# A decoder layer's gate and up projections as Strassen block products: one Trainium2 core

## The chip, the core and the metric

One core of a Trainium2 chip. The metric is device microseconds (us) of one execution. The kernel is written with a tile framework: the program gives instructions in an order of priority, and a scheduler that knows each tile's readers and writers fixes, before the run, the order of instructions on every engine and DMA queue and puts in the semaphores.

## The reference

One layer of a hybrid decoder (two attention kinds, cross-attention into memory tokens, a feed-forward block) on 1024 prompt tokens and 8 sample tokens. What the change touches is the end of it, with D_MODEL = 1024 and D_FF = 2816:

```python
x = x + mem_attend(rmsnorm(x, xattn_norm_g), mem_k, mem_v, w_mq, mq_norm_g, w_mo)
hf = rmsnorm(x, ffn_norm_g)
x = x + (jax.nn.silu(hf @ w_gate) * (hf @ w_up)) @ w_down
```

## The kernel before

Activations lie transposed in SBUF: `xT` is [128 features, 8 blocks, 1032 tokens] in f32. Precision is kept by splitting every operand into a high and a low part (fp32r), and each product of 128 x 128 weights with a group of tokens is three matmuls into one PSUM bank (`proj`, L128): high by high, high by low, low by high. Tokens come in groups of 512, 256 and 264 (`GROUPS2`). A weight tile goes by `load_w` (L112): a DMA on SP's queue into `raw`, a copy on ACT (`wh`, L124) and a subtraction on GpSimd (`wl`, L125), with two buffers of each. `split` (L141) makes the halves of an activation with a copy on ACT and a subtraction on VectorE.

After the attention part, `stage_mem` (L1706) runs four kinds of generators that take turns (`run`): `mem_q`, `mem_attend` (as `both`), `mem_out`, and `mem_sample` for the sample tokens. `mem_out` (L1634) multiplies by `w_mo`, adds to `xT` (`residual`, L1484, with a running sum of squares `sqacc` on GpSimd, L1490), and for each group calls `scaled` (L1492): AH and AL become the halves of `xT` times the gain (L1498 on ACT, L1499 on VectorE), and a matmul of the squares, an Ln and an Exp give `rs`, the row of 1/rms. The norm is applied late: `gate_up` (L1734) multiplies each PSUM result by `rs` (L1745, L1753). So matmuls can start before `rs` is there.

D_FF is 22 tiles f of 128 columns. `gate_up(f)` makes 3 x 8 matmuls for each token group, first with `w_gate`, then with `w_up`; then SiLU (ACT), a product, and `split` into a tile for the down projection. The first 512 tokens of f = 0 to 3 are done beside `both(2, 3)` and `mem_sample`, their other groups after `mem_out(1, 2)`. `stage_ffn` (L1788) then alternates: `down` (L1758) of up to four finished tiles f (for each of 8 output blocks o a weight tile, three groups, one addition each into `xT`, L1767), and `gate_up` of the next four. The last chunk has two tiles f; in it `store_y` (L1771) transposes each finished block o back and stores it.

Of the kernel before, what the change touches and what calls it, by code (L numbers as in the profile page):

```python
# [6 lines left out]
F32 = mybir.dt.float32  # L7
FR = mybir.dt.float32r
# [5 lines left out]
OP = mybir.AluOpType  # L14
AX = mybir.AxisListType
PSUM = bass.MemoryType.PSUM
# [3 lines left out]
T = 1024  # L20
NS = 8
NT = T + NS
KD = D // 128
GROUPS = ((0, 384), (384, 384), (768, 264))
GROUPS2 = ((0, 512), (512, 256), (768, 264))
UW = 1040
EPS = 1e-6
BIG = 1e30
# [6 lines left out]
def f32(ap):  # L35
    return ap.bitcast(F32)


class Kernel:
    def __init__(self, tc, ins, outs):  # L40
        self.tc, self.nc, self.i, self.o = tc, tc.nc, ins, outs
        self.side, self.G = [], GROUPS
        self.set, self.set_users = None, []


    def mm(self, out, lhsT, rhs, start, stop):
# [5 lines left out]
    def unit(self, name, shape=None, dt=F32):  # L52
        return self.u.tile(shape or [128, UW], dt, name=name, tag="u")

# [1 line left out]
        return self.fp.tile(shape or [128, 388], dt, name=name, tag="f")  # L56

    def bt(self, name, shape=None):
        return self.hp.tile(shape or [128, 512], F32, name=name, tag="b", bufs=self.nB)

    def ht(self, name, shape=None, dt=F32):
        return self.hp.tile(shape or [128, 512], dt, name=name, tag="h")
# [1429 lines left out]
    def scaled(self, g, gain, rs):  # L1492

        nc = self.nc
        g0, n = self.G[g]
        s = slice(g0, g0 + n)
        for k in range(KD):
            nc.scalar.activation(self.AH[:, k, s], self.xT[:, k, s], AF.Copy, scale=gain[:, k:k + 1])  # L1498
            nc.vector.scalar_tensor_tensor(self.AL[:, k, s], self.xT[:, k, s], gain[:, k:k + 1], f32(self.AH[:, k, s]),  # L1499
                                           op0=OP.mult, op1=OP.subtract)  # L1500
        p = self.bank("sc", "pnt")
# [204 lines left out]
    def stage_mem(self):  # L1706


        self.omh, self.oml, self.mq = [self.AH[:, t] for t in range(2)], [self.AL[:, t] for t in range(2)], {}
        self.run([self.stage_out(0), 1.0, 0], [self.stage_mem_kv(), 1.2, 0])  # L1710
        self.run([self.stage_out(1, 2), 1.0, 0], [chain(self.mem_q(0), self.both(0, 1)), 0.4, 0])
        self.run([self.mem_q(1, 2), 1.0, 0], [self.mem_out(0), 1.5, 0])
        self.acts = [{} for _ in range(4)]
        gate_up = lambda *g: chain(*(self.gate_up(f, a, *g) for f, a in enumerate(self.acts)))

        def room(a, *groups):
            u, c = self.unit("a2", [128, 2, 520], FR), 0
            for g in groups:
                n = self.G[g][1]
                a[g] = u[:, 0, c:c + n], u[:, 1, c:c + n]  # L1720
                c += n

        for a in self.acts:
            room(a, 0)
# [3 lines left out]
        self.ub, self.u = self.u, self.tc.alloc_tile_pool(name="uC", bufs=10)  # L1728
        for a in self.acts:
            room(a, 1, 2)  # L1730
        self.run([gate_up(1, 2), 1.0, 0])


    def gate_up(self, f, act, *groups):  # L1734
        nc, V = self.nc, self.nc.vector
        cs = slice(128 * f, 128 * f + 128)
        gw = self.load_w(self.i["w_gate"][0][:, cs], KD, 128)
        uw = self.load_w(self.i["w_up"][0][:, cs], KD, 128)
        sgs = {}
        for g in groups:  # L1740
            g0, n = self.G[g]
            p = self.bank("mm", "pg")
            self.proj(*gw, 0, 128, g, p)
            sgs[g] = sg = self.bt("sg")
            V.tensor_mul(sg[:, :n], p[:, :n], self.rs[:, g0:g0 + n])  # L1745
            self.silu(sg[:, :n], sg[:, :n])
            yield
        for g in groups:
            g0, n = self.G[g]
            p = self.bank("mm", "pu")  # L1750
            self.proj(*uw, 0, 128, g, p)
            a = self.bt("a")
            V.tensor_mul(a[:, :n], p[:, :n], self.rs[:, g0:g0 + n])  # L1753
            V.tensor_mul(a[:, :n], a[:, :n], sgs[g][:, :n])
            self.split(a[:, :n], *act[g])
            yield

    def down(self, f0, acts, last):  # L1758
        nc, V = self.nc, self.nc.vector
        kt = len(acts)  # L1760
        for o in range(KD):
            wh, wl = self.load_w(self.i["w_down"][0][128 * f0:128 * (f0 + kt), 128 * o:128 * o + 128], kt, 128)
            for g, (g0, n) in enumerate(self.G):
                p = self.bank(("sc", "sk")[g % 2], "pd")
                self.proj(wh, wl, 0, 128, g, p, kt=kt, act=lambda k: acts[k][g])
                x = self.xT[:, o, g0:g0 + n]
                V.tensor_add(x, x, p[:, :n])  # L1767
            if last:
                self.store_y(o)

    def store_y(self, o):  # L1771
        nc = self.nc
        cs = slice(128 * o, 128 * o + 128)
        for half in range(2):
            p = self.bank(("tp", "sk")[half], "py")
# [3 lines left out]
            y = self.ub.tile([128, 4, 128], F32, name="y", tag="u")  # L1779
            (nc.vector.tensor_copy if half else nc.scalar.copy)(y, p.rearrange("p (t c) -> p t c", c=128))  # L1780
            nc.sync.dma_start(self.o["y_prompt"][0, 512 * half:512 * half + 512, cs].rearrange("(t p) c -> p t c", p=128), y)
        p = self.bank("tp", "py")
        self.tr(p[:NS, :128], self.xT[:, o, T:NT], 128)
        y = self.bt("y", [NS, 128])
# [3 lines left out]
    def stage_ffn(self):  # L1788
        F, C = 22, 4

        def gate_up(f):
            h, l = self.unit("ah", None, FR), self.unit("al", None, FR)
            act = [(h[:, g0:g0 + n], l[:, g0:g0 + n]) for g0, n in self.G]
            for _ in self.gate_up(f, act, 0, 1, 2):
                pass
            return act

        acts, f0 = self.acts, 0
        while f0 < F:
            n = len(acts)  # L1800
            nxt = []
            if f0 + n < F:
                nxt.append(gate_up(f0 + n))
            self.down(f0, acts, f0 + n >= F)
            f0 += n
            while nxt and len(nxt) < C and f0 + len(nxt) < F:
                nxt.append(gate_up(f0 + len(nxt)))
            acts = nxt


    def build(self):
        tc, nc = self.tc, self.nc
        P = tc.alloc_tile_pool
# [58 lines left out]
        self.nb = {"mm": 3, "tp": 1, "sc": 2, "sk": 2}  # L1872
        self.ps = P(name="psB", bufs=1, space=PSUM)
        self.wp = P(name="wB", bufs=1, side="right")
        self.keep = P(name="keepB", bufs=1)
# [4 lines left out]
        self.nB, self.G = 6, GROUPS2  # L1880
        self.u = P(name="uB", bufs=5)
# [5 lines left out]
        self.stage_ffn()  # L1887
        for p in (self.wp, self.u, self.ub, self.hp, self.sm, self.keep, self.act, self.c, self.dr, self.ps):
            p.release()

    def sample_gen(self):
# [33 lines left out]
```

## Time and profile before

| what | value |
|---|---|
| median of 3 runs | 1818.66 us (1818.63 to 1819.53) |
| the profiled execution | 1817.93 us, its span 1816.2 us |
| mean granted TensorE clock | 0.963 |
| busy: PE, PEld, DVE, ACT, POOL | 93%, 81%, 57%, 46%, 36% of the span |
| moved by DMA | 151.42 MB, 83 GB/s on average |

PE is TensorE's matmuls, PEld its weight loads (beside the matmuls), DVE is VectorE, POOL is GpSimd, SP issues most DMAs. A record of a matmul is longer than its share of the array, since matmuls are pipelined: what one costs is read from the distance between starts. The feed-forward block takes the last 800 us, and the engine that matters there is read from the view by stretches and the chain of waits.

### The profile page before, as it was taken

The numbers are of one execution on the slowest core, as the hardware profiler recorded it, in microseconds if no ns is written. First come the engines' busy times: TensorE is split into PE (matmuls) and PEld (weight loads), VectorE is DVE, ScalarE is ACT, GpSimd is POOL, SyncE is SP. The second block draws the span as 40 slices with busy tenths as digits, with TensorE's granted clock in tenths as the row PEclk, the third lists the DMA queues.
The fourth block names the chain that finished last, engine by engine and source line by source line (L and its number), as shares of the span: only waits on it lengthen the run. The fifth ranks groups of instructions, "written<-read, shape, count | busy, mean of one in ns | idle before, by whom it ended". The sixth has DMA issues, their size and how long they took to land.

```text
span 1816.2 us, 30619 instructions
## 1 busy us (share of the span) xinstructions
PE 1681.2 (93%) x11316; PEld 1471.5 (81%) x11316; DVE 1042.8 (57%) x2813; ACT 836.4 (46%) x2033; POOL 659.6 (36%) x641
## 2 busy tenths in 40 slices
PE   6998998767869999989998999999999999999998
PEld 5997887656747777767887779999999999999997
DVE  6799997999769877752366355323323323323324
ACT  5667879763446667645566563112112112112112
POOL 1376663445148133225454444222122122122121
PEclk9999998868989999989999999999999999999999
DMA  4133343323342334356222322121121121121013
GB/s 153 50 107 112 112 148 122 105 71 108 123 123 64 80 81 113 100 156 172 83 82 59 93 78 74 46 61 47 33 61 47 31 64 47 30 64 47 30 50 108
DMA packets 229855, 151.42 MB, mean 83 GB/s; under 512 B 29621, under 2 KB 216202, under 8 KB 229698
## 3 DMA queue, kind: packets, MB, share of 16 engines
q1 hardware_dynamic: 210906, 120.38, 22.9%
q0 software_dynamic: 4864, 14.69, 2.8%
q10 hardware_dynamic: 13936, 14.40, 2.3%
q8 instruction: 89, 1.46, 0.3%
q14 instruction: 60, 0.49, 0.1%
HBM read 118.77 MB, written 30.76 MB: 82 GB/s over the span
## 4 chain that ended last, share of the span: by engine, by line
PE 68%; DVE 11%; issue 3%; ACT 2%; DMA 1%; POOL 0%; SPq 0%; ACTq 0%; DVEq 0%; POOLq 0%
PE pu L47 14%; PE pd L47 14%; PE pg L47 14%; PE pm L47 8%; PE po L47 2%; PE pch L47 2%; PE plg L47 2%; PE pt L50 2%; DVE sk_junk L1266 2%; DVE AL L1499 1%; PE halves L47 1%; DVE tkj L349 1%; PE pmq L47 1%; PE pmo L47 1%; PE pmk L47 1%
## 5 line engine op out<-in xcount | busy, mean ns | idle before, releaser
L125 POOL TENSOR_TENSOR wl<-raw,wh 128x1024 fp32r<-128x1024 f32 (+3 forms) x153 | 311.9, 2039 | 745.8 <-ACT wh L124 741.0
L124 ACT CAST wh<-raw 128x1024 fp32r<-128x1024 f32 (+3 forms) x153 | 137.9, 901 | 311.9 <-PE pd L47 200.0
L47 PE MATMUL pm<-AH,wh 128*128 128x384 f32 (+7 forms) x792 | 270.1, 341 | 7.2 <-ACT wh L124 4.0
L47 PE MATMUL pm<-AL,wh 128*128 128x384 f32 (+7 forms) x792 | 263.4, 333 | 0.1
L47 PE MATMUL pm<-AH,wl 128*128 128x384 f32 (+7 forms) x792 | 262.3, 332 | 0.1
L47 PE MATMUL pg<-AL,wh 128*128 128x512 f32 (+2 forms) x528 | 169.7, 322 | 3.2 <-DVE AL L1499 3.1
L47 PE MATMUL pg<-AH,wh 128*128 128x512 f32 (+2 forms) x528 | 169.9, 322 | 1.1 <-DVE a L1753 1.1
L1767 DVE TENSOR_TENSOR xT<-xT,pd 128x512 f32<-128x512 f32 (+2 forms) x144 | 73.1, 512 | 169.5 <-PE pd L47 168.9
L47 PE MATMUL pu<-AL,wh 128*128 128x512 f32 (+2 forms) x528 | 169.5, 321 | 0.0
L47 PE MATMUL pu<-AH,wh 128*128 128x512 f32 (+2 forms) x528 | 169.4, 321 | 0.0
L47 PE MATMUL pu<-AH,wl 128*128 128x512 f32 (+2 forms) x528 | 168.8, 320 | 0.0
L47 PE MATMUL pg<-AH,wl 128*128 128x512 f32 (+2 forms) x528 | 168.8, 322 | 0.0
L47 PEld LDWEIGHTS pm<-AH,wh 128*128 128x128 f32 (+1 forms) x792 | 154.6, 195 | 15.3 <-ACT wh L124 5.4
L47 PEld LDWEIGHTS pm<-AL,wh 128*128 128x128 f32 (+1 forms) x792 | 154.4, 195 | 6.9 <-issue 1.3
L47 PEld LDWEIGHTS pm<-AH,wl 128*128 128x128 f32 (+1 forms) x792 | 153.6, 194 | 5.9 <-issue 1.1
L47 PE MATMUL pd<-ah,wh 128*128 128x512 f32 (+2 forms) x432 | 139.2, 323 | 0.0
L47 PE MATMUL pd<-al,wh 128*128 128x512 f32 (+2 forms) x432 | 138.3, 320 | 0.0
L47 PE MATMUL pd<-ah,wl 128*128 128x512 f32 (+2 forms) x432 | 137.7, 320 | 0.0
L1745 DVE TENSOR_TENSOR sg<-pg,rs 128x256 f32<-128x256 f32 (+2 forms) x66 | 34.0, 515 | 151.0 <-PE pg L47 142.3
L47 PEld LDWEIGHTS pg<-AL,wh 128*128 128x128 f32 x528 | 100.1, 190 | 11.8 <-DVE AL L1499 4.3
L47 PEld LDWEIGHTS pg<-AH,wh 128*128 128x128 f32 x528 | 100.0, 189 | 9.5 <-DVE a L1753 1.4
L1753 DVE TENSOR_TENSOR a<-pu,rs 128x256 f32<-128x256 f32 (+2 forms) x66 | 34.0, 516 | 128.2 <-PE pu L47 128.2
(647 smaller groups left out, 4196.8 us busy)
## 6 DMA issues: line engine op xcount, KB each, us to landing
raw<-in_w_gate SPq DMA_DIRECT2D x26, 512.0 KB
raw<-in_w_up SPq DMA_DIRECT2D x26, 512.0 KB
raw<-in_w_in SPq DMA_DIRECT2D x24, 512.0 KB
raw<-in_w_down SPq DMA_DIRECT2D x40, 256.0 KB
raw<-in_w_out SPq DMA_DIRECT2D x16, 512.0 KB
scrG<-y ACTq DMA_DIRECT2D x32, 192.0 KB
x<-in_x_prompt SPq DMA_DIRECT2D x8, 512.0 KB
xn<-in_x_prompt SPq DMA_DIRECT2D x8, 512.0 KB
```

What stands on the lines that cost most here:

```text
L47: return self.nc.tensor.matmul(out, lhsT, rhs, start=start, stop=stop)
L50: return self.nc.tensor.transpose(out, in_, self.ident[:p, :p])
L124: self.nc.scalar.copy(wh, raw)
L125: self.nc.gpsimd.tensor_sub(wl, raw, f32(wh))
L349: V.tensor_scalar(junk()[:, :(i + 1) * 128], data[i], t[:, j:j + 1], None, op0=op, op1=OP.add, accum_out=cnt[:, j:j + 1])
L1266: V.tensor_scalar(junk[:, j % 4, :N], data[:, :N], t, None, op0=op, op1=OP.add, accum_out=cnt[:, j:j + 1])
L1499: nc.vector.scalar_tensor_tensor(self.AL[:, k, s], self.xT[:, k, s], gain[:, k:k + 1], f32(self.AH[:, k, s]), op0=OP.mult, op1=OP.subtract)
L1745: V.tensor_mul(sg[:, :n], p[:, :n], self.rs[:, g0:g0 + n])
L1753: V.tensor_mul(a[:, :n], p[:, :n], self.rs[:, g0:g0 + n])
L1767: V.tensor_add(x, x, p[:, :n])
```

## The change

Gate and up use Strassen's scheme (Winograd's form) on 2 x 2 blocks. For a unit u of 256 columns of D_FF (11 units), the weights are four blocks of 512 x 128 (a11, a12, a21, a22: halves of D_MODEL by halves of the columns) and the activations four blocks of 512 features by 512 or 520 tokens (`HN` = 512; the first half is padded to 520 where blocks are combined). Seven block products take the place of eight. Two of them need only plain weights and the first 512 tokens: they are made early, beside cross-attention (`early`), and kept in memory (`scrS`). Five use sums of blocks: of activations, made once (`combine`), and of weights, made for each unit (`unit_product`). `xT` is stored to memory meanwhile. Products of gate and up go to memory (`scrF`), and the down projection is a stage behind all units, in parts of 8, 7 and 7 tiles f (`stage_down`), the first of them split by tokens. `self.E` is 0, so all 11 units are early, and the branches under `if not early` are never taken.

```diff
+    def normed(self, out, k, s):
+        self.nc.vector.scalar_tensor_tensor(out, self.xT[:, k, s], self.g_f[:, k:k + 1], self.rs[:, s], op0=OP.mult, op1=OP.mult)
...
                 if t:
-                    self.scaled(g, self.g_f, self.rs)
+                    self.rms(g, self.rs)
+                    if g == 0:
+                        for k in range(KD):
+                            x = self.bt("xf")[:, :HN]
+                            self.normed(x, k, slice(0, HN))
+                            self.split(x, self.AH[:, k, 0:HN], self.AL[:, k, 0:HN])
...
-        self.run([gate_up(0), 1.5, 0], [self.both(2, 3), 1.0, 0], [self.mem_sample(), 6.0, 0])
+        E = self.E
+        self.run([chain(*(self.early(u) for u in range(E, E + 6))), 2.0, 0], [self.both(2, 3), 1.0, 0], [self.mem_sample(), 6.0, 0])
         self.run([self.mem_out(1, 2), 1.0, 0])
         self.mkp.release()
...
-        self.run([gate_up(1, 2), 1.0, 0])
+        self.tp = self.tc.alloc_tile_pool(name="T", bufs=1, side="right")
+        self.T = {t: tuple(self.tp.tile([128, 4, HN + NS], FR, name=f"T{t}{x}") for x in "hl") for t in (2, 3, 4)}
+        self.run([self.combine(), 1.0, 0], [chain(*(self.early(u) for u in range(E + 6, 11))), 3.0, 0])
+        self.nc.sync.dma_start(self.scrT, self.xT)
+    def combine(self):
...
+        for k in range(4):
+            x12, x22, t2 = (self.bt(x) for x in ("x12", "x22", "t2"))
+            for x in (x11, x21):
+                G.memset(x[:, HN:], 0.0)
+            self.normed(x12, k, n2)
+            self.normed(x11[:, :HN], k, n1)
+            self.normed(x22, k + 4, n2)
+            G.tensor_sub(x11, x12, x11)
+            V.tensor_sub(t2, x22, x11)
+            self.normed(x21[:, :HN], k + 4, n1)
+            G.tensor_sub(x12, x22, x12)
+            G.tensor_sub(x21, x21, t2)
+            self.split(x22, self.AH[:, k + 4, n2], self.AL[:, k + 4, n2])
+            self.split(x11, self.AH[:, k, n2], self.AL[:, k, n2])
+            for t, x in ((2, t2), (3, x12), (4, x21)):
+                self.split(x, self.T[t][0][:, k], self.T[t][1][:, k])
+            yield
+    def early(self, u):
...
+        for j, kind in enumerate(("gate", "up")):
+            w = self.load_w(self.i["w_" + kind][0][:, cs], KD, 128)
+            p = self.bank("mm", "pg")
+            self.corner(*w, p, 0)
+            self.keep_p1(s1[:, j], p)
+            if j:
+                self.nc.sync.dma_start(self.scrS[u - self.E], s1)
+            yield
+            p = self.bank("mm", "pg")
+            self.corner(*w, p, 1)
+            self.first(u, kind, s1[:, j, :HN], p, sg)
+            yield
+    def unit_product(self, u):
...
+        for kind in ("gate", "up"):
...
+            t1 = total(a21, a22, V.tensor_add)
+            t2 = total(t1, a11)
+            t4 = total(a12, t2)
+            halve(2, t2)
+            halve(1, t1)
+            halve(3, total(a11, a21))
+            halve(5, a22)
+            halve(4, t4)
...
+            plus(u1, s1, product(2, "T2", "p6"))
...
+            p5 = product(1, "T1", "p5")
+            plus(u2, u1, product(3, "T3", "p7"))
+            plus(u1, u1, p5)
+            plus(s1, u2, p5)
+            plus(u2, u2, product(5, "T4", "p4"))
+            plus(u1, u1, product(4, "B22", "p3"))
+            c = [u1, u2[:, :HN], s1]
+            if kind == "gate":
+                for x in c:
+                    self.silu(x, x)
+                sg["c"] = c
+            else:
+                f = 2 * u
+                for x, y, dst in zip(c, sg["c"], (self.scrF[f, :, HN:], self.scrF[f + 1, :, 0:HN], self.scrF[f + 1, :, HN:])):
+                    nc.gpsimd.tensor_mul(x, x, y)
+                    nc.sync.dma_start(dst, x)
...
+    def stage_down(self, after_units):
+        acts = [(self.AH[:, k], self.AL[:, k]) for k in range(KD)]
+        n1, n2, n = slice(0, HN), slice(HN, NT), slice(0, NT)
+        for f in range(8):
+            self.fetch(f, *acts[f], n1)
+        after_units()
+        for o in range(KD):
+            self.nc.sync.dma_start(self.xT[:, o, n1], self.scrT[:, o, n1])
+        for f in range(8):
+            self.fetch(f, *acts[f], n2)
+        self.down(0, acts, (0,))
...
+        self.down(0, acts, (1, 2))
...
+        self.down(8, more, (0, 1, 2))
...
+        self.down(15, acts[:7], (0, 1, 2), True)
```

What the cuts leave out: `corner(w, p, j)` is 12 matmuls of 512 tokens on half j of the features; `keep_p1` copies a result on ACT; `first` adds the two early results (VectorE) and makes SiLU or the product (GpSimd) for `scrF`; `total` is one VectorE operation on 128 x 512 into a tile with 3 buffers; `halve` is a copy on ACT and a subtraction on GpSimd of 128 x 512 (7 buffers); `product` is 2 banks of 12 matmuls of 260 tokens; `plus` is two VectorE additions of 128 x 260 from PSUM; `fetch` loads a tile f from `scrF` and splits it. Behind `stage_mem` the pools of `xT`, `rs` and the small tiles are released, one PSUM pool of 8 banks takes the place of the four tags, and the tiles of the weight sums are put where `xT` was; `after_units` releases these and puts `xT` back.

## Rows read from the trace of the kernel before

**Rows 1.** The page: busy time, share and instructions; the chain by engine.
```profile
PE 1681.2 (93%) x11316; PEld 1471.5 (81%) x11316; DVE 1042.8 (57%) x2813; ACT 836.4 (46%) x2033; POOL 659.6 (36%) x641
...
PE 68%; DVE 11%; issue 3%; ACT 2%; DMA 1%; POOL 0%; SPq 0%; ACTq 0%; DVEq 0%; POOLq 0%
```

**Rows 2.** View by stretches: us, busy time (instructions) of each engine, PEclk, DMA.
```profile
990.00:1010.00 20.00, 20.00 (x108) 16.48 (x107) 14.11 (x19) 12.10 (x22) 11.91 (x6) 1.00 0.28 80
...
1010.00:1097.00 87.00, 80.95 (x507) 63.95 (x505) 45.00 (x87) 53.27 (x120) 40.48 (x33) 1.00 0.27 80
...
1142.70:1779.00 636.30, 636.30 (x4033) 576.06 (x4032) 199.94 (x336) 112.44 (x184) 137.25 (x76) 1.00 0.16 46
1779.00:1816.20 37.20, 31.96 (x218) 27.97 (x216) 18.53 (x35) 10.00 (x24) 5.15 (x7) 0.98 0.46 132
```

**Rows 3.** Chain that ended last, in order of time: start, us, what.
```profile
1131.19 5.77 PE pg L47 x48
...
1142.73 11.35 PE pg L47 x72
...
1781.75 0.44 PE py L50 x4
```

**Rows 4.** Timeline of PE, 1300 to 1310: start, us, operation.
```profile
1301.58 0.39 PE L47 MATMUL pd<-ah,wh 128*128 128x512 f32 x1
...
1304.36 0.28 PE L47 MATMUL pd<-ah,wh 128*128 128x256 f32 x1
...
1305.78 0.29 PE L47 MATMUL pd<-ah,wh 128*128 128x264 f32 x1
```

**Rows 5.** Timeline of DVE, 960 to 1100.
```profile
977.55 7.32 DVE L1499 SCALAR_TENSOR_TENSOR AL<-xT,vc,AH 128x512 fp32r<-128x512 f32 x2
...
989.49 0.75 DVE L1499 SCALAR_TENSOR_TENSOR AL<-xT,vc,AH 128x512 fp32r<-128x512 f32 x1
```

**Rows 6.** Groups by form, 1000 to 1820: count, busy us, mean ns, idle before.
```profile
L125 POOL TENSOR_TENSOR wl<-raw,wh 128x512 fp32r<-128x512 f32 x40 | 52.4, 1309 | 224.0 <-ACT wh L124 224.0
L124 ACT CAST wh<-raw 128x512 fp32r<-128x512 f32 x40 | 24.9, 622 | 164.9 <-PE pd L47 147.7 <-PE pg L47 9.9 <-PE pu L47 7.4
L1767 DVE TENSOR_TENSOR xT<-xT,pd 128x264 f32<-128x264 f32 x48 | 20.6, 429 | 36.4 <-PE pd L47 36.4
L1754 DVE TENSOR_TENSOR a<-a,sg 128x512 f32<-128x512 f32 x22 | 15.1, 691 | 2.3 <-DVE a L1753 0.5
```

**Rows 7.** Timeline of ACT, 970 to 1100.
```profile
1008.31 0.69 ACT L107 ACTIVATE rs<-pnt,eps 128x512 f32<-128x512 f32 x1 [0.16 <-PE pnt L47]
```

**Rows 8.** PE's groups by line and operation, 990 to 1010: count, busy us, mean ns.
```profile
L47 PE MATMUL pg<-AH,wh 128*128 128x512 f32 x10 | 3.9, 394 | 0.0
```

**Rows 9.** Timeline of DVE, 1195 to 1262.
```profile
1195.23 0.42 DVE L1767 TENSOR_TENSOR xT<-xT,pd 128x256 f32<-128x256 f32 x1 [0.99 <-PE pd L47]
...
1234.00 0.43 DVE L1754 TENSOR_TENSOR a<-a,sg 128x264 f32<-128x264 f32 x1
1234.91 2.36 DVE L143 TENSOR_TENSOR al<-a,ah 128x264 fp32r<-128x264 f32 x1 [0.48 <-ACT ah L142]
```

**Rows 10.** Timeline of POOL, 1195 to 1262.
```profile
1194.42 1.30 POOL L125 TENSOR_TENSOR wl<-raw,wh 128x512 fp32r<-128x512 f32 x1 [4.37 <-ACT wh L124]
...
1234.58 2.41 POOL L125 TENSOR_TENSOR wl<-raw,wh 128x1024 fp32r<-128x1024 f32 x1 [8.97 <-ACT wh L124]
```

**Rows 11.** DMA view, 1225 to 1238 in 40 slices: GB/s in each.
```profile
GB/s 0 0 0 0 0 72 95 268 339 347 350 144 0 0 0 0 0 0 0 0 0 0 0 0 0 0 0 0 50 0 0 0 0 0 0 0 0 0 0 0
```

**Rows 12.** Timeline of SP's queue, 1690 to 1817: first issue, us to the last, count.
```profile
1754.30 26.45 SPq L114 DMA_DIRECT2D raw<-in_w_down  x4
1782.84 0.38 SPq L1781 DMA_DIRECT2D out_y_prompt<-y  x1
1785.04 0.37 SPq L114 DMA_DIRECT2D raw<-in_w_down  x1
...
1795.37 17.63 SPq L1781 DMA_DIRECT2D out_y_prompt<-y  x12
```

More of the change, by code (lines that the diff above doesn't have):

```diff
@@ L25 @@
 GROUPS2 = ((0, 512), (512, 256), (768, 264))
+HN = 512
 UW = 1040
@@ L42, in __init__ @@
         self.side, self.G = [], GROUPS
-        self.set, self.set_users = None, []
+        self.set, self.set_users, self.bw = None, [], 512
     def mm(self, out, lhsT, rhs, start, stop):
@@ L58, in bt @@
     def bt(self, name, shape=None):
-        return self.hp.tile(shape or [128, 512], F32, name=name, tag="b", bufs=self.nB)
+        return self.hp.tile(shape or [128, self.bw], F32, name=name, tag="b", bufs=self.nB)
     def ht(self, name, shape=None, dt=F32):
@@ L1712, in stage_mem @@
         self.run([self.mem_q(1, 2), 1.0, 0], [self.mem_out(0), 1.5, 0])
[L1713 to L1724, printed above, removed]
@@ L1758, in down @@
-    def down(self, f0, acts, last):
+        self.tp = self.tc.alloc_tile_pool(name="T", bufs=1, side="right")
[3 more added lines that the diff above has]
+    def combine(self):
+        G, V = self.nc.gpsimd, self.nc.vector
+        w = HN + NS
+        n1, n2 = slice(0, HN), slice(HN, HN + w)
+        xx = self.unit("xx", [128, 2, w])
+        x11, x21 = xx[:, 0], xx[:, 1]
+        for k in range(4):
[15 more added lines that the diff above has]
+            yield
@@ new lines, in corner, with three, keep_p1 @@
+    def corner(self, wh, wl, p, j):
+        for k in range(4 * j, 4 * j + 4):
+            self.three(p, wh[:, k], wl[:, k], self.AH[:, k, :HN], self.AL[:, k, :HN], k % 4 == 0, k % 4 == 3)
+    def three(self, p, h, l, ah, al, first, last):
+        self.mm(p, h, ah, first, False)
+        self.mm(p, h, al, False, False)
+        self.mm(p, l, ah, False, last)
+    def keep_p1(self, s1, p):
+        self.nc.gpsimd.memset(s1[:, HN:], 0.0)
+        self.nc.scalar.copy(s1[:, :HN], p)
+    def early(self, u):
+        cs, s1 = slice(256 * u, 256 * u + 128), self.unit("s1", [128, 2, HN + NS])
+        sg = self.unit("sg", [128, 2, HN])
+        for j, kind in enumerate(("gate", "up")):
[10 more added lines that the diff above has]
+            yield
@@ L1759, in down @@
+    def down(self, f0, acts, groups, last=False):
         nc, V = self.nc, self.nc.vector
@@ L1774, in store_y @@
         for half in range(2):
-            p = self.bank(("tp", "sk")[half], "py")
+            p = self.bank("g", "py")
             for t in range(4):
@@ L1783, in store_y, with fetch @@
         self.tr(p[:NS, :128], self.xT[:, o, T:NT], 128)
-        y = self.bt("y", [NS, 128])
+        y = self.unit("y8", [NS, 128])
         nc.scalar.copy(y, p[:NS, :128])
         nc.scalar.dma_start(self.o["y_sample"].rearrange("b o d -> (b o) d")[:, cs], y)
[L1788 to L1808, printed above, removed]
+    def fetch(self, f, h, l, s):
+        a = self.unit("af")[:, :s.stop - s.start]
+        self.nc.sync.dma_start(a, self.scrF[f, :, s])
+        self.split(a, h[:, s], l[:, s])
@@ new lines, in stage_down @@
+    def stage_down(self, after_units):
[9 more added lines that the diff above has]
+        self.down(0, acts, (0,))
+        for o in range(KD):
+            self.nc.sync.dma_start(self.xT[:, o, n2], self.scrT[:, o, n2])
+        self.down(0, acts, (1, 2))
+        more = [[self.du.tile([128, UW], FR, name="d" + x, tag="d")[:, :NT] for x in "hl"] for _ in range(7)]
+        for f in range(8, 15):
+            self.fetch(f, *more[f - 8], n)
+        self.down(8, more, (0, 1, 2))
+        for f in range(15, 22):
+            self.fetch(f, *acts[f - 15], n)
+        self.down(15, acts[:7], (0, 1, 2), True)
@@ L1874, in build @@
         self.wp = P(name="wB", bufs=1, side="right")
+        self.u = P(name="uB", bufs=5)
+        self.scrT, self.scrF = self.dr.tile([128, KD, NT], F32, name="scrT"), self.dr.tile([22, 128, NT], F32, name="scrF")
+        self.E, self.scrS = 0, self.dr.tile([11, 128, 2, HN + NS], F32, name="scrS")
         self.keep = P(name="keepB", bufs=1)
@@ L1886, in build, with after_units @@
         self.stage_mem()
-        self.stage_ffn()
-        for p in (self.wp, self.u, self.ub, self.hp, self.sm, self.keep, self.act, self.c, self.dr, self.ps):
+        for p in (self.hp, self.sm, self.keep):
+            p.release()
+        self.ps.release()
+        self.nb = {"g": 8}
+        self.ps = P(name="psG", bufs=1, space=PSUM)
+        self.gv = P(name="gv", bufs=1)
+        self.gw = P(name="gw", bufs=1)
+        for u in range(11):
+            self.unit_product(u)
+        def after_units():
+            for p in (self.tp, self.gw, self.gv):
+                p.release()
+            self.keep = P(name="keepD", bufs=1)
+            self.xT = self.keep.tile([128, KD, NT], F32, name="xT")
+            self.du = P(name="du", bufs=14)
+        self.stage_down(after_units)
+        for p in (self.wp, self.du, self.keep, self.u, self.act, self.c, self.dr, self.ps):
             p.release()
```

107 lines of the change are left out of this document (75 added, 32 removed).

## Prediction

> **What bounds the kernel now.** I began with the page: matmuls fill 93% of the span, and two thirds of the chain that ended last are TensorE [rows 1]. That is an average, so next came the view by stretches. From 1142.7 to 1779 us TensorE is busy for all 636.3 of 636.3 us at a granted clock of 1.00, the higher of its two levels, while VectorE has 200 us of work, ScalarE 112 and GpSimd 137 [rows 2]. In that stretch only fewer or shorter matmuls count; work taken from or given to another engine is free as long as it stays under TensorE's. Before it, from 1010 to 1097 (cross-attention beside the first gate and up tiles), TensorE idles 87.0 - 80.95 = 6.0 us; the last 37.2 us end in transposes and stores [rows 2].
>
> The chain gives prices: 72 matmuls of one kind and one tile f take 11.35 us, 48 of 256 and 264 columns 5.77 us [rows 3]. The timeline splits it: twelve of 512 columns from 1301.58 to 1304.36, 0.2317 us each; twelve of 256 to 1305.78, 0.1183 each [rows 4]. Matmuls of 260 columns do not occur; midway between 256 and 264 they cost 5.77 / 48 = 0.1202 us [rows 3]. So the price goes with the columns, and a half-size matmul costs 52% of a whole one.
>
> **Gate and up: fewer columns.** Before: 44 pairs (tile f, kind) at 11.35 to 11.37 us, 500 us. After: 22 pairs (unit, kind), each with 24 matmuls of 512 columns (the early products) and 120 of 260 (five products, two banks, 12 each): 24 x 0.2317 + 120 x 0.1202 = 19.98 us, together 439.6. **Term: -60.7 us.** The count of matmuls is unchanged (144 per pair of tiles and kind). Against this speaks a rule of the Trainium skill, "TensorE: Matmul & The Clock Gate", section "Back-to-back issue gap": in a stream of weight load and matmul it gives 81 ns for 128 columns and 131 ns for 512. A line through the two, an estimate, makes 98 ns at 260, and the saving would be 17 us; the trace has 232 and 120 and decides.
>
> **A wait for the norm.** The early products need normalized activations, since sums of blocks cannot be scaled afterwards. Now a first matmul waits for `rs`, then for eight blocks each with `normed` and a subtraction on VectorE (0.75 + 0.69 us [rows 5, 6]): 11.5 us. Before, `rs` started to be made at 1008.31 [rows 7], and 28 pg and 24 pu matmuls of 512 (the row shown, two more pg groups of 9, three pu groups of 8) had already begun between 990 and 1010 [rows 8]: 12.0 us of filling that is not there any more. In return L1499 leaves VectorE: two of them took 7.32 us instead of 2 x 0.75 [rows 5], with the additions that free `mem_out`'s banks behind them. The residual, its sum of squares and `rs` should come some 8 us earlier. I take half of the lost filling, **+6 us**; the ends are 0 (`rs` 12 us earlier) and +24 (no earlier: 12.0 + 11.5).
>
> **Filling in cross-attention.** Early products beside and behind `mem_out(1, 2)` do not need its result, where the old gate tiles of groups 1 and 2 did. **-6 us**, all the idle time there; the other end is 0.
>
> **The combination.** `combine` has per k four `normed`, one `t2` and five subtractions of splits on VectorE, all with two SBUF inputs, and three subtractions on GpSimd. Four k: 16 x 0.75 + 24 x 0.69 = 28.6 us of VectorE, 12 x 1.31 = 15.7 us of GpSimd [rows 5, 6]. TensorE's cover is `early` of units 6 to 10, 20 steps of 12 x 0.2317 = 2.78 us, 55.6 us, less about 8 that run in the gaps of `mem_out`: 48. Whether it is enough hangs on one thing. VectorE's addition from PSUM took 0.42 us under a running GpSimd subtraction [rows 9, 10], its usual price. But the subtraction of two SBUF tiles took 2.36 us when it started 0.33 us after a GpSimd operation of 2.41, against 0.43 for the same size just before [rows 9, 10]: it stood until GpSimd was done. So I add the two engines: 28.6 + 15.7 + about five weight splits (2.41 each) and two products (1.31) of `early` that stand between in the order, 14.7, makes 59, less what ACT's copies let through. Then unit 0 needs two totals, a copy and a subtraction, 3.3 us. 59 + 3 - 48 = 14, **+15 us** with the clock's return. The low end is 0 (side by side, 28.6 us lie under the 48), the high end +40 (all ten splits, 24.1, in front, and ACT's copies not hidden). The Trainium skill, "SBUF — State Buffer", section "Who interferes with whom", says that a VectorE instruction with two SBUF inputs and a GpSimd instruction that reads SBUF exclude each other for a whole instruction; the trace agrees with its 2.36 us. By it the sum is this 15, without it 0.
>
> The store of `xT` is 4.2 MB. A weight load reached 339 to 350 GB/s [rows 11], so 12 us of the queue; `early` has two weight tiles ready, 11 us. Taken as 0, at worst +12. The weight sums of unit 0 lie where `xT` was and wait for it too, beside the combination.
>
> **Units.** Per kind TensorE has 120 x 0.1202 = 14.4 us. VectorE: twelve additions from PSUM at 0.43 and four totals at 0.69, 7.9 us. ACT: five copies at 0.62 and in gate kinds three SiLU of that size, 5.0 at most. GpSimd: five subtractions of 1.31, 6.6, in up kinds three products more, 10.5 [rows 6]. GpSimd with the totals: 9.3 and 13.3 us, under 14.4, but in up kinds not by much. DMA: 2 MB of weights, 0.5 of `scrS`, 0.8 of stores per 28.8 us, 115 GB/s. Eight banks let VectorE be four products late. **+5 us** for starts; the ends are 0 and +29, a GpSimd operation of 1.31 in each of 22 kinds. All stalls would show at the first matmul of a kind.
>
> **Down.** As many matmuls as before. `w_down` for the first part is loaded twice, eight loads of 512 KB with a copy and a split: hidden, with 5.6 us of matmul per block for 2.4 us of GpSimd; without that cover it would be 8 x 3 us. Loads of `scrF` and of `xT` raise the DMA to about 18 MB in 90 us, 203 GB/s, under the 339. Only the first 512 tokens of eight f are needed at the start, ready long before. **+2 us**, at worst +10. The tail: 37.2 us [rows 2] for 2 x 11.35 of matmul and 72 transposes at 0.11 [rows 3], 30.6; 6.6 us are waits between short blocks. With seven tiles f a block lasts 9.9 us and only the last one shows. **-3.5 us**, between 0 and -6.6.
>
> **Sum.** -60.7 + 6 - 6 + 15 + 5 + 2 - 3.5 = -42.2. The profiled execution took 1817.93 us, 0.73 under the median; 1775.7 there, 1776.5 as a median. Of this kernel 0.2% (3.6 us) can be told from no change.
>
> **Rivals.**
> - *Everything is covered* (0.17). Norm and combination cost nothing: 1776.5 - 21 = 1755. For it speaks the 6 us that `mem_out` lost to L1499; against it the 2.36 us.
> - *VectorE and GpSimd shut each other out further* (0.15): combination +40, units +15: 1811. For it speak the up kinds, 13.3 of 14.4.
> - *Stores stand in front of the loads on SP's queue* (0.11), the slower one. The three stores of a unit wait for its last product; if the next unit's weights are queued behind, TensorE waits for a 1 MB load (4 us), two totals, copy and subtraction (3.3), queueing (2), some 9.5 us, at ten boundaries: 1776.5 + 95 = 1871. It turns slower from 4.2 us per boundary. Against it: in the tail, where each block's loads stand in the program behind the stores of the block before, four loads were issued before the first store, and more between stores [rows 12]; the order follows readiness as the scheduler expects it.
> - *Short matmuls alone don't keep 0.1202* (0.05), for 2640 in a row. If weight loads set 0.136, the gain is gone: 1819. The Trainium skill's page above ("TensorE: Matmul & The Clock Gate") says that both operations set the spacing. Against it: 48 in a row held 0.1202 [rows 3].
> - *The change repeats what it meant to move* (0.02): with the early products made again in the units, +122: 1899. `E` = 0 excludes it as I read it.
>
> **Numbers.** The forecast has 0.50. Faster: 0.50 + 0.17 + 0.15 = 0.82; within 0.2%: 0.05; slower: 0.11 + 0.02 = 0.13. The range reaches from a little under full cover, 1745 (with the low ends of units and tail), to the second rival, 1812; 2 in 10 lie outside.
>
> **What would show it.** A pair (unit, kind) of 14.4 us in the chain, 120 matmuls of 260 columns at 0.120; a gap of TensorE between the last early product and the first p6 of about 15 us, ended by GpSimd or VectorE; a gap before the first early product at about 1000; no `raw` issue right behind a `scrF` store with TensorE idle. Wrong would be: a distance between starts over 0.125 in the units, a gap at each unit, or a down stage over 250 us plus its transposes.

## The result and the profile after

The change makes the kernel faster by about half of what was forecast: 1797.79 us as the median of four runs (1797.03 to 1799.69), against 1819.1 for the kernel before in runs on the same chip, a ratio of 0.9883 with a 95% interval of 0.9866 to 0.99. The forecast was 1776.5, a gain of 42; the gain is 21.3. The profiled span went from 1816.2 to 1795.4 us.

The page, busy time by engine, answers to [rows 1]: TensorE has the same 11316 matmuls in less time, every other engine has more work.

```profile
PE 1635.1 (91%) x11316; PEld 1444.1 (80%) x11316; DVE 1110.0 (62%) x2913; ACT 881.5 (49%) x2069; POOL 831.3 (46%) x791
```

The view by stretches of the kernel after, with the columns of [rows 2]; the first two lines and the last answer to the same stretches there:

```profile
990.00:1010.00 20.00, 14.36 (x72) 8.48 (x71) 13.67 (x24) 13.57 (x25) 10.53 (x10) 0.83 0.23 67
1010.00:1097.00 87.00, 82.22 (x441) 65.43 (x441) 25.02 (x54) 47.62 (x94) 32.48 (x29) 0.96 0.37 119
...
1121.00:1137.00 16.00, 16.00 (x72) 13.03 (x71) 1.94 (x4) 6.13 (x11) 10.58 (x13) 1.00 0.97 360
...
1150.00:1160.00 10.00, 6.23 (x21) 4.70 (x20) 10.00 (x9) 4.06 (x6) 7.52 (x5) 0.83 0.39 121
1160.00:1170.00 10.00, 9.59 (x42) 7.42 (x40) 9.96 (x10) 4.52 (x8) 7.23 (x9) 1.00 0.36 107
1170.00:1180.00 10.00, 6.90 (x23) 5.53 (x24) 9.96 (x8) 3.69 (x6) 9.38 (x8) 0.83 0.25 79
1180.00:1190.00 10.00, 6.97 (x25) 5.22 (x24) 9.96 (x10) 3.70 (x6) 6.85 (x6) 0.83 0.39 115
...
1270.70:1469.50 198.80, 198.76 (x1658) 198.77 (x1659) 123.20 (x233) 57.30 (x99) 122.76 (x91) 1.00 0.42 131
1521.00:1566.00 45.00, 37.92 (x151) 28.85 (x149) 20.70 (x23) 15.60 (x17) 17.03 (x9) 0.93 0.90 316
...
1780.00:1795.40 15.40, 11.24 (x75) 9.90 (x72) 2.92 (x5) 1.36 (x4) 0.00 (x0) 0.98 0.25 71
```

Before, TensorE was full from 1142.7 on. Now it stands still in three places: at 990 to 1010 (14.36 of 20), from 1140 to 1200, where VectorE is the full engine (9.96 to 10 of 10 from 1150 to 1190), and at 1521 to 1566, where the DMA engines are at 0.90. In the first two the mean granted clock of a slice falls to 0.83, so part of it ran at the lower level (1.2 GHz). Of the units between, the 198.8 us shown are full, with DVE and POOL at 62%. The last stretch starts at another point of the work than the one before (31.96 of 37.20), so the tail is compared in the table.

To price the places I took, for each two neighbouring matmuls of a trace, the distance between their starts less the median distance of the first one's shape, and added up by stretch what lies above zero. This is the time that TensorE lost to waits or a lower clock, with some scatter (4.7 us came out before in a stretch where TensorE was full):

| stretch (us; before / after) | lost before | lost after | change forecast | found |
|---|---|---|---|---|
| 960 to the first gate matmul (996.3 / 1008.4) | 9.5 | 15.6 | +6 (norm) | +6.1 |
| to the feed-forward stage (1142.7) / the combination (1139.8) | 16.8 | 13.2 | -6 (filling) | -3.6 |
| the combination to the first p (1199.2) | none | 21.1 | +15 | +21.1 |
| 45 us from the first pd (1521.1) | none | 11.0 | +2 | +11.0 |
| units, and the rest of down to 1780 | 4.7 | 8.0 + 3.7 | +5 | +7.0 |
| tail | 3.8 | 0.2 | -3.5 | -3.6 |
| sum | 34.8 | 72.8 | +18.5 | +38.0 |

At the median distances of the two traces (0.232, 0.118 and 0.122 us for 512, 256 and 264 columns before; 0.232 and 0.120 for 512 and 260 after) the matmuls of gate and up make -59.1, and with the losses -21.1; the spans differ by 20.8. So the losses missed their forecast by 19.5 us: 9 at the start of down, 6 at the combination, 2.4 in the filling, 2 in the units.

**The combination, closer.** VectorE's timeline of the kernel after, 1139 to 1199; L1805 and L1808 are the early products' additions, the other lines the combination:

```profile
1139.20 0.69 DVE L1805 TENSOR_TENSOR sg<-s,pg 128x512 f32<-128x512 f32 x1 [5.85 <-ACT wh L125]
...
1145.66 4.60 DVE L1513 SCALAR_TENSOR_TENSOR x<-xT,vc,rs 128x520 f32<-128x520 f32 x2
...
1151.91 0.69 DVE L144 TENSOR_TENSOR AL<-xx,AH 128x520 fp32r<-128x520 f32 x1
...
1153.13 2.84 DVE L144 TENSOR_TENSOR AL<-x,AH 128x520 fp32r<-128x520 f32 x1
1155.90 0.67 DVE L1808 TENSOR_TENSOR sg<-s,pg 128x512 f32<-128x512 f32 x1
...
1161.35 0.68 DVE L1805 TENSOR_TENSOR sg<-s,pg 128x512 f32<-128x512 f32 x1
...
1172.28 0.67 DVE L1808 TENSOR_TENSOR sg<-s,pg 128x512 f32<-128x512 f32 x1
```

GpSimd's timeline of the same kernel:

```profile
1145.14 2.84 POOL L126 TENSOR_TENSOR wl<-raw,wh 128x1024 fp32r<-128x1024 f32 x1
...
1152.78 2.64 POOL L126 TENSOR_TENSOR wl<-raw,wh 128x1024 fp32r<-128x1024 f32 x1
```

A subtraction of 0.69 us took 2.84 when it started 0.35 us after GpSimd's split and ended 0.55 us behind it. The additions from PSUM keep 0.67, but they stand in VectorE's order behind such operations: 16.7 us lie between the first two, 10.9 between the third and the fourth. Each frees the PSUM bank of an early product, and so does ACT's copy `s` (L1782), in turn. The view of waits, PE from 1139 to 1203, names them:

```profile
PE pg L48 <- DVE sg L1808: 7.3, 2, 3.8
PE pg L48 <- ACT s L1782: 3.0, 1, 3.0
PE p L48 <- ACT sh L1841: 2.8, 1, 2.8
```

(Us waited, times, longest.) These three are 13.1 of the 21.1. After each wait for L1808 or L1782 the matmuls of 512 columns at first start 0.43 us apart instead of 0.23, in slices whose granted clock was 0.83; 20 such distances make 3.9 us more, and two waits for GpSimd's `wl` 1.6. The wait for ACT goes back to VectorE too, as ACT's timeline of the kernel after shows:

```profile
1182.82 0.63 ACT L143 CAST AH<-x 128x520 fp32r<-128x520 f32 x1 [3.89 <-DVE x L1513]
1183.35 0.58 ACT L1782 COPY s<-pg 128x512 f32<-128x512 f32 x1
```

**The start of down, closer.** SP's queue in the kernel after:

```profile
1528.56 5.07 SPq L1937 DMA_DIRECT2D af<-scrF  x3
1534.74 4.06 SPq L1948 DMA_DIRECT2D xT<-scrT  x8
...
1542.52 0.38 SPq L115 DMA_DIRECT2D raw<-in_w_down  x1
1543.15 3.47 SPq L1953 DMA_DIRECT2D xT<-scrT  x4
1547.03 4.16 SPq L1937 DMA_DIRECT2D af<-scrF  x5
```

The view of DMAs from 1521 to 1566 in 40 slices, GB/s in each:

```profile
GB/s 364 252 244 70 191 88 374 393 356 319 400 427 418 415 407 395 388 388 406 363 302 351 396 358 301 349 396 413 385 411 396 418 415 343 296 291 147 20 0 0
```

The chain that ended last, of the kernel after (start, us, what):

```profile
1270.74 198.77 PE p L48 x1656
...
1542.52 7.61 DMA raw<-in_w_down
...
1553.79 10.35 DMA raw<-in_w_down
```

14.2 MB came in these 45 us, 12.7 of them in 34 us at 376 GB/s on average. Two weight loads of 512 KB took 7.6 and 10.4 us in it from issue to landing; the bytes of the load in [rows 11] moved within seven slices of 0.325 us, 2.3 us.

### The profile page after: what moved, and what is told of

It reads as the page before. It is cut to its first block, busy times and chain, and to the rows that moved or that the text cites. A ratio compares the mean times of both kernels' runs of the same rounds, so it can differ in the third digit from the quotient of the medians.

```text
span 1795.4 us, 31553 instructions
## 1 busy us (share of the span) xinstructions
PE 1635.1 (91%) x11316; PEld 1444.1 (80%) x11316; DVE 1110.0 (62%) x2913; ACT 881.5 (49%) x2069; POOL 831.3 (46%) x791
## 5 line engine op out<-in xcount | busy, mean ns | idle before, releaser
L126 POOL TENSOR_TENSOR wl<-raw,wh 128x1024 fp32r<-128x1024 f32 (+2 forms) x107 | 256.2, 2396 | 406.7 <-ACT wh L125 334.9
L125 ACT CAST wh<-raw 128x1024 fp32r<-128x1024 f32 (+2 forms) x107 | 109.9, 1028 | 253.1 <-PE pd L48 166.7
L1842 POOL TENSOR_TENSOR sl<-S,sh 128x512 fp32r<-128x512 f32 x88 | 119.5, 1368 | 89.6 <-ACT sh L1841 89.6
L48 PE MATMUL pd<-AH,wh 128*128 128x512 f32 (+2 forms) x360 | 117.1, 327 | 4.4 <-ACT wh L125 4.4
L48 PE MATMUL pd<-AH,wl 128*128 128x512 f32 (+2 forms) x360 | 116.3, 325 | 2.6 <-POOL wl L126 2.6
L48 PE MATMUL pd<-AL,wh 128*128 128x512 f32 (+2 forms) x360 | 116.0, 323 | 0.0
L48 PE MATMUL p<-AL,sh 128*128 128x260 f32 x352 | 99.8, 284 | 0.0
L48 PE MATMUL p<-AH,sh 128*128 128x260 f32 x352 | 99.7, 283 | 0.0
L48 PE MATMUL p<-AH,sl 128*128 128x260 f32 x352 | 99.3, 283 | 0.0
L48 PE MATMUL pg<-AH,wh 128*128 128x512 f32 x176 | 74.2, 424 | 14.4 <-DVE sg L1808 7.3
```

What stands on the lines that cost most here:

```text
L48: return self.nc.tensor.matmul(out, lhsT, rhs, start=start, stop=stop)
L125: self.nc.scalar.copy(wh, raw)
L126: self.nc.gpsimd.tensor_sub(wl, raw, f32(wh))
L1842: nc.gpsimd.tensor_sub(l, x, f32(h))
```

## Experiments

Lost time below is by the method of the table; "in the combination" runs from its first VectorE operation of 520 columns (1139.8 in the kernel after; two of 512 columns ran earlier, at 1105) to the first p, the combination's length from there to its last VectorE operation; "at down" is the 45 us from the first pd. The ratio is to the kernel before on the same chip, whose median was 1816.5 to 1817.6 in these groups.

**The norm.** The first token group's early products from activations that are not scaled by 1/rms:

```diff
-                    self.rms(g, self.rs)
                     if g == 0:
-                        for k in range(KD):
...
+                        self.scaled(g, self.g_f, self.rs)
+                    else:
+                        self.rms(g, self.rs)
```

> The first 512 tokens are scaled by the gain alone, as before the change, and not by 1/rms: this leaves out the normalization of the early products' operand. Theory (the first early product waits for the norm, first pg at 1008 us against 996 before): the first pg comes at 994 to 998 us, and the time falls by 6 to 12 us, to 1786 to 1792. Rival (the matmuls of cross-attention fill the wait, since they came forward): the time within 3 us of 1798.

Measured: 1789.28 us, ratio 0.984 [0.9814, 0.9866]. The first early matmul starts at 997.7 instead of 1008.4, the loss before it falls from 15.6 to 9.3, and the loss in the combination stays (21.1). So the wait for the norm cost 6.3 us in this pair of traces: the forecast's +6. In the other runs, which wait for the norm as the change does, a stretch of the same length before the first early matmul lost 15.7 to 17.7 us, so the price may be some 2 us higher.

**The start of down.** The seven loads of the second part wait, each for a copy of one column into its buffer:

```diff
+        if after is not None:
+            self.nc.vector.tensor_copy(a[:, 0:1], after)
         self.nc.sync.dma_start(a, self.scrF[f, :, s])
...
-            self.fetch(f, *more[f - 8], n)
+            self.fetch(f, *more[f - 8], n, self.xT[:, f - 8, 0:1])
```

> The loads of the seven tiles of the second down part wait for the additions of the first (one more VectorE copy of one column each), instead of being issued at once behind the units. Theory (4 MB of them stand in the DMA queue in front of the weights of the first down blocks): of the 11 us that TensorE loses between 1521 and 1566 us some 5 to 8 go, the time falls to 1790 to 1793 us. Rival (the last gate and up products and the other loads, xT and the first tiles, are enough to fill the queue, or the copies and subtractions of the tiles hold the weights' halves): the loss stays 9 to 11 us and the time within 3 us of 1798.

Measured: 1788.72 us, ratio 0.9829 [0.9801, 0.9857]. Lost at down: 5.0 instead of 11.0; in the rest of it 2.4 instead of 3.7. The stretch in this run, which answers to 1521 to 1566 above:

```profile
1520.40:1565.40 45.00, 40.98 (x175) 32.11 (x174) 22.00 (x30) 13.89 (x15) 18.86 (x9) 1.00 0.79 263
```

175 matmuls instead of 151, DMA share 0.79 instead of 0.90, the clock full. So 6 of the 11 us came from bulk loads that nobody needed yet, beside the loads that TensorE waited for.

**Cover, order and banks.** Four runs asked whether the combination lacks early matmuls to lie under (x1: two more units kept for it), whether the scheduler puts them too late (x5: a larger share in the turn-taking), both (x6), or whether their three PSUM banks are too few (x7: cover and banks of two more kinds).

```diff
-        self.run([chain(*(self.early(u) for u in range(E, E + 6))), 2.0, 0], [self.both(2, 3), 1.0, 0], [self.mem_sample(), 6.0, 0])
+        self.run([chain(*(self.early(u) for u in range(E, E + 4))), 2.0, 0], [self.both(2, 3), 1.0, 0], [self.mem_sample(), 6.0, 0])
...
-        self.run([self.combine(), 1.0, 0], [chain(*(self.early(u) for u in range(E + 6, 11))), 3.0, 0])
+        self.run([self.combine(), 1.0, 0], [chain(*(self.early(u) for u in range(E + 4, 11))), 5.0, 0])
```

x1 has the new ranges with 3.0, x5 the old ones with 5.0, x6 both as shown; x7 is x1 with the banks of `early` taken in turn from "mm", "sc", "mm", "sk".

> Four early units instead of six beside cross-attention, seven instead of five beside the combination. Theory (the combination takes some 58 us of VectorE and GpSimd, and the changed kernel has only 40 us of early matmuls left when it starts): the combination starts some 20 us earlier, keeps its length, and now has about 60 us of matmuls beside it; the 24 us that TensorE loses between 1137 and 1202 us fall to under 8, and the time to 1780 to 1785 us. Rival A (early matmuls slow down beside the combination whatever their number, because their additions stand in VectorE's queue behind it): the loss stays about 24 us and the time within 4 us of 1798. Rival B (cross-attention then lacks filling): what is gained there is lost between 1008 and 1100, the time again 1795 to 1800.

> Only the share of early steps between the four steps of the combination changes, from 3 to 5; six early units still lie beside cross-attention. Theory (two things bind at once: the order of VectorE's queue lets only three early products pass per step of 14.5 us, and only 38 us of early matmuls are left for 58 us): without more cover the loss of 21 us between the combination's start and the first unit product stays at 18 to 23, and the ratio to the kernel before within 0.002 of 0.988. Rival (the order alone binds): the loss falls under 12 us, the ratio under 0.984.

> Five early steps per step of the combination, and seven early units beside it instead of five. Theory: 65 us of early matmuls stand beside 58 to 62 us of combination, and none waits behind more than a fifth of a step; the loss between the combination's start and the first unit product falls from 21 to 23 us to under 9, the ratio to the kernel before to 0.978 to 0.982. Rival (early products are held by something else beside the combination, ScalarE's copies or the weight halves on GpSimd): the loss stays over 17 us and the ratio at 0.986 to 0.988, as with the cover alone.

> The seven early units beside the combination, at the old share of three steps, with seven PSUM banks instead of three (those of two idle tags). Theory (early products wait for banks, since the additions that free them stand behind a step of the combination): with four banks more TensorE runs some 11 us ahead, and the loss falls from 23 us to 8 to 14, the ratio from 0.987 to 0.981 to 0.984. Rival (the order of the combination's steps sets the pace of the early products however many banks there are, because weights and copies stand in the same order on ScalarE and GpSimd): the loss stays over 18 us.

| run | us | ratio | combination, us | early matmul time left at its start | lost in it |
|---|---|---|---|---|---|
| after | 1797.79 | 0.9883 [0.9866, 0.99] | 58.0 | 38.2 | 21.1 |
| x1 | 1794.63 | 0.987 [0.9848, 0.9892] | 55.0 | 64.9 | 23.0 |
| x5 | 1796.24 | 0.9885 [0.9867, 0.9903] | 58.0 | 38.2 | 21.1 |
| x6 | 1796.79 | 0.9876 [0.9859, 0.9894] | 54.8 | 64.9 | 22.5 |
| x7 | 1798.1 | 0.9886 [0.9869, 0.9902] | 56.0 | 68.1 | 20.1 |

None of them can be told from the change itself: x5 came out as its theory had it (two limits at once), in x1, x6 and x7 the theory failed. (x1's profile is of its longest execution, 1807.78 us; x6 shows nearly the same.) With 64.9 us of matmuls for 55 us of combination, TensorE still loses 23, and the rest of the early matmuls runs after the combination. So cover alone doesn't help. The waits and a stretch of x6, whose VectorE made only five additions L1805 or L1808 in the first 49 us:

```profile
PE pg L48 <- DVE sg L1805: 8.1, 2, 6.3
PE pg L48 <- DVE sg L1808: 5.1, 1, 5.1
...
1125.00:1135.00 10.00, 5.58 (x18) 4.53 (x19) 10.00 (x9) 3.24 (x5) 6.18 (x7) 0.66 0.27 76
```

Nine operations fill VectorE's 10 us, and TensorE gets 18 matmuls.

x7 has banks enough: no wait of TensorE for a bank is left. It waits for the halves of the weights instead, made on GpSimd and ACT (x7, 1116 to 1173), and loses 20.1 all the same:

```profile
PE pg L48 <- POOL wl L126: 9.1, 4, 3.1
PE pg L48 <- ACT wh L125: 3.9, 2, 3.2
```

So the banks are only the first thing that runs out; the engines of the combination owe the early products their weights too.

**The exclusion.** x2 moves the combination's three GpSimd subtractions to VectorE. x9 moves besides the weight splits and products of `early` from unit 6 on, so that GpSimd has nothing that reads SBUF in this stretch; x10 is x9 with the ranges of x1 (and from unit 4 on).

```diff
-            G.tensor_sub(x11, x12, x11)
+            V.tensor_sub(x11, x12, x11)
...
-            w = self.load_w(self.i["w_" + kind][0][:, cs], KD, 128)
+            eng = self.nc.vector if u >= 6 else self.nc.gpsimd
+            w = self.load_w(self.i["w_" + kind][0][:, cs], KD, 128, eng)
...
-            self.nc.gpsimd.tensor_mul(sg[:, 1], sg[:, 0], sg[:, 1])
+            (eng or self.nc.gpsimd).tensor_mul(sg[:, 1], sg[:, 0], sg[:, 1])
```

> The twelve GpSimd subtractions of the combination go to VectorE. Theory (the two engines exclude each other, so their times add): twelve operations of 1.75 us on GpSimd become twelve of 0.69 on VectorE and the locked ones get shorter, the combination falls from 58 to about 47 us, the time by 8 to 11 us to about 1788. Rival (VectorE's own work is the length, GpSimd runs beside it): VectorE gets 8 us more, the combination 58 to 66 us, the time 1798 to 1806 us.

> Beside the combination GpSimd gets no instruction that reads SBUF: the combination's subtractions, and the weight halves and products of the five early units there, go to VectorE; six early units stay beside cross-attention. Theory (the order on VectorE was fixed for operations of 0.69 us, and the exclusion of the two engines stretches them to 1 to 2.5 us, so that the early additions in between come late by the same factor): operations take 0.7 us again, VectorE has about 53 us of work for the stretch, and TensorE 38 us of early matmuls: the loss falls from 21 to 15 to 19 us, ratio 0.984 to 0.987. Rival (no exclusion; VectorE is simply the busier engine): 24 us more on VectorE, the stretch 75 to 80 us, the ratio 0.995 to 1.000.

> The same with seven early units beside the combination. Theory: 65 us of early matmuls beside some 57 us of VectorE work that runs at the pace for which the order was made: the loss between the combination's start and the first unit product falls from 23 (cover alone) to under 9 us, the ratio to 0.976 to 0.981. Rival (it is the cover's order in the program that holds the early products, not the stretching): the loss stays over 15 us, the ratio 0.984 to 0.988.

| run | us | ratio | combination, us | early matmul time left | lost in it |
|---|---|---|---|---|---|
| x2 | 1789.4 | 0.9838 [0.9815, 0.9862] | 52.2 | 38.2 | 16.6 |
| x9 | 1782.38 | 0.9808 [0.9783, 0.9832] | 50.3 | 46.6 | 6.2 |
| x10 | 1781.29 | 0.9804 [0.9777, 0.9832] | 48.8 | 69.5 | 5.9 |

VectorE's groups by form in the combination, first of the kernel after (1139 to 1198), then of x9 (1127 to 1180): count, busy us, mean ns.

```profile
L1513 DVE SCALAR_TENSOR_TENSOR x<-xT,vc,rs 128x520 f32<-128x520 f32 x8 | 15.7, 1996 | 0.0
L144 DVE TENSOR_TENSOR AL<-x,AH 128x520 fp32r<-128x520 f32 x4 | 8.2, 2042 | 0.0
L144 DVE TENSOR_TENSOR T4l<-xx,T4h 128x520 fp32r<-128x520 f32 x4 | 6.5, 1633 | 0.0
```

```profile
L126 DVE TENSOR_TENSOR wl<-raw,wh 128x1024 fp32r<-128x1024 f32 x7 | 8.5, 1221 | 0.2
L1513 DVE SCALAR_TENSOR_TENSOR x<-xT,vc,rs 128x520 f32<-128x520 f32 x8 | 5.7, 755 | 1.9 <-ACT rs L105 1.9
...
L144 DVE TENSOR_TENSOR T4l<-xx,T4h 128x520 fp32r<-128x520 f32 x4 | 2.8, 696 | 1.2 <-ACT T4h L143 1.2
L144 DVE TENSOR_TENSOR AL<-x,AH 128x520 fp32r<-128x520 f32 x4 | 2.8, 696 | 0.0
```

x2 refutes its rival (the combination gets shorter), but 52.2 us is not the 47 of its theory. In x2 the gain is smaller than in x9, and GpSimd still reads SBUF there for the weight splits and products of `early`. In x9 the same operations take 0.70 to 0.76 us instead of 1.6 to 2.0, and the combination is 7.7 us shorter though VectorE took over GpSimd's work. (x9's profile is of its shortest execution, 1775.86 us; x10's is at its median.) x9 came out better than its theory, 6.2 us lost for 15 to 19. The waits of PE fall to two, none of them for a bank (x9, 1127 to 1181):

```profile
PE p L48 <- ACT sh L1842: 2.1, 1, 2.1
PE pg L48 <- DVE wl L126: 1.9, 1, 1.9
```

x9 alone doesn't show that early products run faster, since it also has more cover left (46.6 us for 38.2) and a shorter combination: 50.3 + 2.6 to the first p - 46.6 = 6.3, for the 6.2 found. x10 against x1 shows it, since both have more cover than combination. The stretches of the two combinations, x1 and x10:

```profile
1123.00:1178.00 55.00, 39.94 (x145) 30.49 (x144) 53.58 (x43) 24.87 (x39) 41.37 (x33) 0.84 0.35 113
1111.20:1160.00 48.80, 46.89 (x196) 37.52 (x195) 47.87 (x70) 28.19 (x43) 1.19 (x14) 0.97 0.59 180
```

The columns are those of [rows 2]. TensorE gets 196 matmuls in 48.8 us instead of 145 in 55, with VectorE nearly full in both. Against x9, x10's extra cover adds nothing to the time.

**Together.** x8 is x6, x2 and x3, and x11 is x10 and x3, both with the reload of the second half of `xT` held in the same way:

```diff
         for o in range(KD):
+            self.nc.vector.tensor_copy(self.xT[:, o, HN:HN + 1], self.xT[:, o, 0:1])
             self.nc.sync.dma_start(self.xT[:, o, n2], self.scrT[:, o, n2])
```

> All together: four early units beside cross-attention and seven beside the combination at five steps, the combination's subtractions on VectorE, and the loads of the second down part and of the second half of xT held until additions of the first part. Theory: the gains add, 13 to 17 us from cover and order, 3 to 6 from the subtractions, 6 to 9 from the loads: a ratio of 0.972 to 0.977 to the kernel before, some 1767 to 1777 us. Rival (with the combination covered, its length costs nothing and the subtractions give nothing more): 0.976 to 0.979.

> The last one with the held loads of the down stage. Theory: the held loads gave 0.005 alone, the two add: ratio 0.970 to 0.976, 1762 to 1774 us. Rival (they overlap): 0.977 to 0.980, as the first combination.

x8: 1782.58 us, ratio 0.9796 [0.9775, 0.9816], lost 16.1 in the combination and 2.1 at down; it missed its theory (1767 to 1777 us), which counted on 13 to 17 us from cover and order that x6 did not bring. x11: 1767.96 us, ratio 0.974 [0.9704, 0.9775], lost 5.6 and 3.5, and the best version found: 2.6% under the kernel before. TensorE has no gap in its combination past 1125:

```profile
1125.00:1135.00 10.00, 10.00 (x45) 8.10 (x44) 10.00 (x16) 4.77 (x8) 0.24 (x3) 1.00 0.28 91
1135.00:1145.00 10.00, 10.00 (x45) 8.12 (x44) 10.00 (x15) 5.46 (x9) 0.35 (x4) 1.00 0.57 172
```

VectorE is as full as in x6, with 16 and 15 operations in 10 us instead of 9.

## Why the prediction was wrong

**Right: the matmuls.** "A half-size matmul costs 52% of a whole one" held: the chain has 1656 of 260 columns in 198.77 us, 0.1200 each (0.1202 forecast). The 2640 of all units took 321.9 us. The term is -59.1 at the measured distances, for -60.7. The rival that short matmuls alone don't keep this price is refuted. The spacing that the Trainium skill gives ("TensorE: Matmul & The Clock Gate", section "Back-to-back issue gap"), by which the saving was estimated at 17 us, does not hold for these matmuls: 232 ns at 512 columns, 120 at 260.

**Right: the norm wait.** +6 forecast, +6.1 found, 6.3 by x4. That it fits so closely is luck, since half of the lost filling was a choice between 0 and +24. `rs` was indeed earlier, by 6.1 us for the forecast's 8; ACT's timeline of the kernel after, against 1008.31 in [rows 7]:

```profile
1002.22 0.69 ACT L108 ACTIVATE rs<-pnt,eps 128x512 f32<-128x512 f32 x1
```

**Right: tail, units nearly, SP's queue.** Tail -3.6 for -3.5. Units and rest of down lost 2 us more than forecast, with no wait at every unit: the 1656 matmuls in a row span almost seven units of 240. The rival of stores ahead of loads did not come: on SP's queue a unit's loads go out between its stores.

```profile
1286.42 3.70 SPq L1826 DMA_DIRECT2D raw<-in_w_up  x2
1292.28 0.34 SPq L1901 DMA_DIRECT2D scrF<-s  x1
...
1300.28 0.38 SPq L1826 DMA_DIRECT2D raw<-in_w_gate  x1
1300.75 0.53 SPq L1901 DMA_DIRECT2D scrF<-uu  x1
```

**Wrong: the combination, "59 + 3 - 48".** The length came out (58.0 for 59), and the Trainium skill's rule that was weighed there ("SBUF — State Buffer", section "Who interferes with whom") holds in this kernel: x9 takes GpSimd's reads away and the operations return to 0.70 to 0.76 us. That the length agrees so well is luck in part: seven weight splits and four products of `early` stood beside it, not five and two, and two of the 16 `normed` ran before it. At the forecast's prices the two engines' work adds up to 65 us (27.1 of VectorE's, 15.7 of subtractions, 16.9 of splits, 5.2 of products), so some 7 of it ran side by side.

The step that failed is "TensorE's cover is `early`", the 48, in two ways. First its size: 17.4 us of the 55.6 ran before the combination, not 8, and 38.2 were left. With that the forecast's own sum gives the loss of this kernel: 58.0 + 1.4 to the first p - 38.2 = 21.2. VectorE is nearly full for the 58, so here early products that come sooner would not have helped. Second, the sum takes the early matmuls as running at full pace beside the combination, so that more of them would cover more. They don't: with 64.9 us left (x1, x6) the loss stays at 23.0 and 22.5, and only when GpSimd's reads are gone does more cover run beside it (x10, 5.9). Early products need additions on VectorE and copies on ACT to free their banks, and weight halves from ACT and GpSimd; all of these stand, in an order fixed before the run, behind operations that the exclusion stretched or that wait for such. The banks bind in the kernel after and in x6, the weight halves in x7. The second rival, VectorE and GpSimd shutting each other out further, names the right place and overstates the price (+40 there, 1811 in all).

How much of it is the length of the stretched operations and how much the order that was fixed for them is not separated: x9 and x10 also change the order and the engine that makes the weight halves. That the scheduler counted with unstretched operations is argued, not shown.

**Wrong: the start of down, "+2, at worst +10".** This is the largest part of the miss. The forecast spread 18 MB over 90 us, 203 GB/s, and held it against the 339 of [rows 11]. The loads came as 14.2 MB in the first 45 us, as soon as their buffers were free, on the queue of `w_down`; TensorE lost 11.0. The step that failed is the comparison of an average rate with a peak: it says nothing of what stands beside an urgent load. x3 takes 6.0 of it back, and x8, with `xT` held too, 8.9. Whether the time goes by shared DMA engines or by the order of issue on SP was not separated.

**Wrong: the filling.** -3.6 instead of -6, "all the idle time there". The step that failed is that early products fill every gap: they wait themselves. Of the 13.2 us still lost there, 3.7 are one early product that waits at 1050 for ACT's copy L1782 to free a bank, and 6.9 lie between early matmuls. No run took this apart.

**Left open.** The first gap (15.6 us lost from 960 on) was priced by x4, not closed in a kernel that computes the whole. The store of `xT` wasn't isolated: the DMA share is 0.97 from 1121 to 1137, and TensorE is busy 16.00 of 16.00 us there, which agrees with the 0 forecast.

## What to carry to other kernels

Work laid under a long stretch of VectorE and GpSimd runs there only at the pace at which these engines serve it. Ask what each of its steps needs from them (a PSUM bank emptied, a weight half made) and where that stands in their order, not only how many microseconds of matmul there are; more banks alone moved the wait to the weight halves. Where VectorE reads two SBUF tiles beside a GpSimd that reads SBUF, giving GpSimd's share to VectorE can shorten both. Loads that nobody needs yet should wait for something late, when urgent weight loads share their queue.

## What the runs showed of the hardware

VectorE doing all of the work (x9) was faster than VectorE and GpSimd sharing it: 50.3 us against 58.0, with seven weight splits of 1.22 us more (GpSimd needed 2.4 to 2.8 for one). GpSimd pays as well; in the groups of the kernel after, from 1139 to 1198, its subtraction of 520 columns took 1.78 us, where one of 512 takes 1.31 in [rows 6]:

```profile
L1762 POOL TENSOR_TENSOR x<-x,x 128x520 f32<-128x520 f32 x4 | 7.1, 1780 | 0.0
```

A standstill cost more than its length: in the combination of the kernel after, the slices with TensorE's waits of 3 to 4 us had a granted clock of 0.83, and behind the waits the matmuls of 512 columns started 0.43 us apart, not 0.23.
